# A decoder layer in three-product fp32 on one core: attention probabilities and half of the gated sum turned by VectorE and DMAs, and two of five FFN pairs computed by seven block products

## Chip, cores and metric

One core of a Trainium2 chip runs the whole layer in one launch. The metric is the device time of one execution in microseconds (us). The kernel before was timed three times, and its median is the number to compare with. Beside the times stands one profiled execution of the kernel before; all rows and durations come from it. Engines are named as the profile names them: PE (TensorE matmul), PEld (its weight loads), DVE (VectorE), ACT (ScalarE), POOL (GpSimd), SP (SyncE, which here only issues DMAs). SPq and ACTq are the queues on which SP and ACT issue DMAs.

## The reference

```python
h = rmsnorm(x, norm1_g)                       # x: 256 tokens x 1024
u = h @ w_in                                  # 1024 x 7168: rnn_x | rnn_gate | q | k | v | two gates
ya = rg_lru(causal_dwconv4(x_rnn)) * gelu(g_rnn)
yb = softmax(causal(rms(q) @ rms(k).T)) @ v   # 8 heads x 128; 256 tokens are one block
merged = sigmoid(g_A) * (ya @ w_proj_rnn) + sigmoid(g_B) * (yb @ w_proj_attn)
x = x + merged @ w_out
h = rmsnorm(x, norm2_g)
up = causal_dwconv3(h @ w_up)                 # 1024 x 2816
x = x + (gelu(up) * (h @ w_gate)) @ w_down    # 2816 x 1024
```

All of it is float32, with one sequence of 256 tokens and one layer.

## The kernel before, in words

**Matmuls.** Each float32 operand is split into two parts of type fp32r: `hi` is a cast (ACT), `lo` is the rest `raw - hi` (DVE). A product is three matmuls, hi*hi, hi*lo and lo*hi (`mm3`, line 424). The weights arrive as chunks of 128 x 2048 (1 MB). SP loads a chunk into `raw`, ACT casts it to `hi`, DVE subtracts to `lo`, and then PE runs 48 matmuls of 512 columns for two chunks of a 512-column weight block: 8 blocks of the inner dimension, 2 token tiles, 3 products. There are 3 buffers for `raw`, 4 for `hi` and 3 for `lo`.

**Stages.** The input projection runs in the order rx, rg, k, q, ga, v, gb with the recurrent gates `ri` between; attention (`att_s` line 772, `att_t` 797, `att_o` 807) is woven into ga, v, gb and pr; then come the projections pr and pa, the output projection `yo`, and the FFN. The FFN has five pairs: pair p is 512 columns of w_up and 512 of w_gate (`up`, `gt`), then a last half pair (`last`) and eleven chunks of w_down (`dn`, accumulated in `acc`).

**Turning.** PE leaves tokens on the partitions; the convolution and the next matmul want channels there. `turn` (line 446) does it without PE: one DVE transpose in 32 x 32 blocks, four DMAs that write the tile to DRAM with the blocks in order, and one DMA that reads it back. SP issues all five, and the read must wait until the writes have landed. The tiles q, k, rx, rg and all FFN outputs are turned so. Three other turns are done by PE with an identity matrix: the probabilities of a head (`pt`, three 128 x 128 transposes in `att_t`), the gated sum (`mT`, `m_t` line 860, four groups of four) and the second norm's input (`h2T`).

**Order.** The kernel's functions only record operations. `Later.issue` (line 283) then emits them in the order of the table `ORDER` (line 160): a number is a recorded operation of ACT, DVE, POOL or SP, and `+n` is the next n matmuls. Each engine runs its own instructions strictly in that order. As one line emits them all, every row of the profile carries L296, and groups are told apart by the names of their tiles.

Of the kernel before, what the change touches and what calls it, by code (L numbers as in the profile page):

```python
# [7 lines left out]
F32 = mybir.dt.float32  # L8
# [6 lines left out]
P = 128  # L15
S = 256
# [13 lines left out]
HALVES, SMALLS, WARM, RAWS = 23, 10, 11, 3  # L30
AHEAD_S, AHEAD_L = 2, 3
DVE_HI = (39, 42, 43)
KEPT = {"upd": 2, "gtd": 2, "u": 1, "c": 2, "ah": 3, "al": 3, "s": 1}
UNITS = ("rx0 rx1 rx2 rx3 rg0 rg1 rg2 rg3 k0 k1 k2 k3 ri0 q0 q1 ri1 ga0 ga1 q2 q3 v0 v1 ga2 ga3 v2 v3 gb0 "
         "gb1 gb2 gb3 pr0 pr1 pr2 pr3 pa0 pa1 pa2 pa3")
AFTER = {
    "rx0.0": "s4 stats",
    "rg0.0": "ev0",
    "rg0.3": "ev1",
    "rg1.1": "rx0",  # L40
    "rg1.2": "s5 rx1",
    "rg1.3": "s6 ge0",
    "rg2.1": "xo0",
    "rg3.0": "rgr0",
    "rg3.1": "conv0",
    "rg3.2": "xo1",
    "rg3.3": "s7 ge1",
    "k0.0": "s8 s9",
    "k0.2": "rgr1 conv1",
    "k1.2": "s10 s11",  # L50
    "k1.3": "s12",
    "k2.2": "s13",
    "k2.3": "split0 decay",
# [96 lines left out]
    "gt41.3": "ur4",  # L150
    "dn4.0": "fu4 s69",
    "dn4.1": "s70 fg3",
    "dn5.2": "lr5 gr4",
    "dn5.3": "s71",
    "dn7.0": "fu fg fg4",
    "dn8.0": "s73",
    "dn9.3": "s74",
}

ORDER = """  # L160
0-2 +1 3-4 +1 5 +1 6 +1 8 +1 7 +1 9 +1 11 +2 10 25 +1 12 30 +1 26-27 +1 14 +1 28 33 +1 29 +1 13 31 +2 32 +2 34 +2
35 +3 15 +6 36 +3 41 +3 19 +2 37 +1 63 42 +1 39 +4 43 38 +1 17 +1 40 +3 44 +1 49 +1 18 +3 45 +1 64 50 +1 47 +3 51
+1 48 +1 16 +1 46 +2 52 +2 57 +4 53 +1 58 +1 55 +3 59 +1 54 +1 56 +3 60 +8 66 +4 68 67 +6 69 +2 99 +3 65 +5 70 +1
100 +4 71 +6 72 98 +1 73 +1 74-75 +1 76 +1 77 +1 78 +1 104 79 +1 80 +1 81 +1 82-83 +5 84 +1 105 +2 85 +3 116 +4 86
# [49 lines left out]
952 +1 951 +1 953 +3 954 +3 956 +1 955 +2 958 +2 957 +2 959-961  # L214
"""


# [972 lines left out]
```

## Time and profile before

| | |
|---|---|
| median of 3 runs | 434.46 us (434.1 to 435.2) |
| span of the profiled execution | 432.3 us from its first to its last instruction |
| around the span, against the median | 434.46 - 432.3 = 2.1 us |
| instructions in the profile | 5409 |
| loaded from and stored to DRAM by DMA | 101.09 MB |

The span is what the views of the profile divide; the 2.1 us around it are taken as unchanged. "Busy" is the time in which at least one instruction of an engine is in flight. Matmuls overlap each other, so a matmul's own duration is longer than its share of PE's time: the share is read from start to start.

### The profile page before, as it was taken

The page shows a single profiled execution, that of the slowest core. Times are in us where ns is not written, and L with a number is a line of the kernel's source. Part 1 is how long each engine was busy: PE and PEld are TensorE (multiplying, and loading weights), DVE is VectorE, ACT ScalarE, POOL GpSimd, SP SyncE. Part 2 cuts the span into 40 slices and gives each one's busy share as a digit, 9 for nine tenths or more (in the row PEclk, how much of TensorE's full clock was granted, in tenths as well). Part 3 has the DMA queues.
Part 4 walks back from the last instruction along what each step waited for, and adds up shares of the span by engine and source line. Part 5 has one row for each costly group of instructions (what it writes and reads, how often), then busy time and mean ns, then how long its engine had stood idle before and what let it go on. Part 6 is the DMA issues. An engine that isn't in the chain of part 4 may idle for free.

```text
span 432.3 us, 5409 instructions
## 1 busy us (share of the span) xinstructions
PE 427.6 (99%) x1992; PEld 357.3 (83%) x1992; DVE 324.5 (75%) x417; ACT 271.2 (63%) x307; POOL 51.9 (12%) x101
## 2 busy tenths in 40 slices
PE   9999999999999999999999999999999999999996
PEld 8888888888887888888888888888888888888885
DVE  4867499899898999865666796587888667769633
ACT  5687596886999998853241364468566556456510
POOL 0022483567160000000000000000000000000000
PEclk9999999999999999999999999999999999999999
DMA  7997945999991844474453556898888688788402
GB/s 253 395 394 256 339 169 149 295 314 335 368 313 38 284 142 149 130 238 134 181 194 116 176 203 207 299 325 253 284 265 313 237 270 262 243 286 293 152 0 97
DMA packets 33833, 101.09 MB, mean 234 GB/s; under 512 B 3216, under 2 KB 14096, under 8 KB 30352
## 3 DMA queue, kind: packets, MB, share of 16 engines
q1 hardware_dynamic: 33664, 100.76, 69.1%
q8 instruction: 15, 0.25, 0.2%
q14 instruction: 10, 0.08, 0.0%
q10 hardware_dynamic: 144, 0.00, 0.0%
HBM read 89.74 MB, written 11.01 MB: 233 GB/s over the span
## 4 chain that ended last, share of the span: by engine, by line
PE 87%; DMA 5%; ACT 3%; DVE 2%; issue 2%; SPq 0%; ACTq 0%; DVEq 0%
PE acc L296 14%; PE up L296 13%; PE gt L296 13%; PE rx L296 5%; PE gb L296 5%; PE pr L296 5%; PE yo L296 5%; PE pa L296 5%; PE k L296 5%; PE rg L296 5%; DMA qm<-qd 3%; PE q L296 3%; PE last L296 3%; PE v L296 2%; DMA raw<-in_win_fm 2%
## 5 line engine op out<-in xcount | busy, mean ns | idle before, releaser
L296 DVE TENSOR_TENSOR lo<-raw,hi 128x2048 fp32r<-128x2048 f32 (+1 forms) x72 | 160.3, 2227 | 40.1 <-PE gt L296 10.5
L296 ACT CAST hi<-raw 128x2048 fp32r<-128x2048 f32 (+1 forms) x69 | 128.3, 1862 | 49.7 <-PE gt L296 11.8
L296 PE MATMUL up<-hi,h2h 128*128 128x512 f32 x80 | 31.3, 391 | 0.0
L296 PE MATMUL up<-hi,h2l 128*128 128x512 f32 x80 | 31.2, 389 | 0.0
L296 PE MATMUL up<-lo,h2h 128*128 128x512 f32 x80 | 31.1, 389 | 0.0
L296 PE MATMUL gt<-hi,h2h 128*128 128x512 f32 x80 | 31.1, 389 | 0.0
L296 PE MATMUL gt<-lo,h2h 128*128 128x512 f32 x80 | 31.1, 389 | 0.0
L296 PE MATMUL gt<-hi,h2l 128*128 128x512 f32 x80 | 31.1, 389 | 0.0
L296 PE MATMUL acc<-hi,fah 128*128 128x512 f32 x80 | 31.1, 389 | 0.0
L296 PE MATMUL acc<-lo,fah 128*128 128x512 f32 x80 | 31.1, 389 | 0.0
L296 PE MATMUL acc<-hi,fal 128*128 128x512 f32 x80 | 31.1, 389 | 0.0
L296 POOL TENSOR_TENSOR rsq<-rsq 128x8 f32<-128x8 f32 x32 | 19.2, 600 | 28.6 <-DVE rsq L296 26.3
L296 ACT ACT_TABLE_LOAD x15 | 19.2, 1283 | 1.4 <-PEq L1180 1.2
L296 DVE SCALAR_TENSOR_TENSOR fc<-fu,pv,fc 128x255 f32<-128x255 f32 (+1 forms) x40 | 17.3, 477 | 2.1 <-ACT fc L296 2.1
L296 ACT ACTIVATE fc<-fu,pv 128x256 f32<-128x256 f32 x20 | 10.8, 593 | 11.1 <-DVE fu L296 11.1
L296 PEld LDWEIGHTS up<-hi,h2l 128*128 128x128 f32 x80 | 15.0, 188 | 3.2
L296 PEld LDWEIGHTS acc<-lo,fah 128*128 128x128 f32 x80 | 15.0, 188 | 3.1
L296 PEld LDWEIGHTS acc<-hi,fal 128*128 128x128 f32 x80 | 15.0, 188 | 3.1
L296 PEld LDWEIGHTS gt<-hi,h2l 128*128 128x128 f32 x80 | 15.0, 188 | 3.1
L296 PEld LDWEIGHTS gt<-lo,h2h 128*128 128x128 f32 x80 | 15.0, 188 | 3.1
L296 PEld LDWEIGHTS gt<-hi,h2h 128*128 128x128 f32 x80 | 15.0, 188 | 3.1
L296 PEld LDWEIGHTS acc<-hi,fah 128*128 128x128 f32 x80 | 15.0, 188 | 3.1
(222 smaller groups left out, 1038.8 us busy)
## 6 DMA issues: line engine op xcount, KB each, us to landing
raw<-in_win_fm SPq DMA_DIRECT2D x12, 1024.0 KB, 7.6
raw<-in_win_tm SPq DMA_DIRECT2D x12, 1024.0 KB, 7.2
raw<-in_wdown SPq DMA_DIRECT2D x11, 1024.0 KB, 6.7
raw<-in_wup SPq DMA_DIRECT2D x10, 1024.0 KB, 5.3
raw<-in_wgate SPq DMA_DIRECT2D x10, 1024.0 KB, 7.3
raw<-in_wpr SPq DMA_DIRECT2D x4, 1024.0 KB, 4.8
raw<-in_wpa SPq DMA_DIRECT2D x4, 1024.0 KB, 4.9
raw<-in_wout SPq DMA_DIRECT2D x4, 1024.0 KB, 4.8
```

The source lines that it names most:

```text
L296: getattr(engine, name)(*map(real, a), **{n: real(v) for n, v in k.items()})
```

## The change

1. **Probabilities.** `att_t` no longer uses PE. DVE transposes the 128 x 384 probabilities in blocks, SP writes them to DRAM in four DMAs, one DMA reads them back, and `att_o` reads the tile with a rearranged view. The 24 identity transposes are gone.
2. **Gated sum.** Its first half (g = 0) is turned by `turn` in `pa_evac`; the second half still uses PE (8 of 16 transposes are gone).
3. **Queue of the reads.** Every read-back of `turn` is issued by ACT (`TURN_ACT = "r"`); the writes stay on SP.
4. **FFN pairs 1 and 3** are computed as a 2 x 2 block product with seven block products instead of eight. The token halves and the two halves of the inner dimension are the blocks of the left operand, up and gate with the two halves of the inner dimension those of the right one. `forms` makes four sums of the left blocks once (for both pairs); `group` makes the sums of weight blocks, two by DVE additions of 128 x 2048 and two by DMAs that POOL issues and that add 1 MB from DRAM onto a loaded chunk. Each of the seven products needs its own split. Three weight chunks are loaded per group, the fourth comes in through the two adding DMAs.
5. **Smaller edits.** The copy of a turned `up` tile moves from DVE to ACT (`FU`); three casts that DVE did (`DVE_HI`) go to ACT; `raw` has 4 buffers instead of 3, the pool of 128 x 1024 tiles 21 instead of 23, the evacuated FFN tile `s` 2 instead of 1; all PSUM banks form one pool of 8. `ORDER` is another table.

```diff
-HALVES, SMALLS, WARM, RAWS = 23, 10, 11, 3
-DVE_HI = (39, 42, 43)
-KEPT = {"upd": 2, "gtd": 2, "u": 1, "c": 2, "ah": 3, "al": 3, "s": 1}
+HALVES, SMALLS, WARM = 21, 10, 11
+BUFS = {"raw": 4, "hi": 4, "lo": 3}
+SUMS = "dvdv"
+TURN_ACT = "r"
+KEPT = {"upd": 2, "gtd": 2, "u": 1, "c": 2, "ah": 3, "al": 3, "s": 2}
 ORDER = """
-0-2 +1 3-4 +1 5 +1 6 +1 8 +1 7 +1 9 +1 11 +2 10 25 +1 12 30 +1 26-27 +1 14 +1 28 33 +1 29 +1 13 31 +2 32 +2 34 +2
...
+0 2 1 3 +3 5 +4 6 +3 8 +1 7 9 11 10 12 14 13 24 15 29 17 25 18 28 +1 26 +1 32 27 +2 30 +3 31 +2 33 +3 34 +9 35 +3 40
...
-        item[read] = lambda: nc.sync.dma_start(dst, mid)
+        (nc.scalar if "r" in TURN_ACT else nc.sync).dma_start(dst if back is None else back, mid)
...
     def att_t(h):
-        sm = heads[h]
-        ps = bank(f"pt{h}")
-        for b in range(3):
-            nc.tensor.transpose(ps[:, b * P:(b + 1) * P], sm[:, b * P:(b + 1) * P], ident)
-        pth, ptl = small(f"pth{h}", 384, F32R), small(f"ptl{h}", 384, F32R)
-        split2(pth, ptl, ps[:, :3 * P])
+        turn(f"pm{h}", small(f"pd{h}", 384), probs[h], 3, probs[h])
+        a = small(f"ph{h}", 384, F32R), small(f"pl{h}", 384, F32R)
+        split2(*a, probs[h])
...
+    def forms(name, hi_, lo_, m, new):
...
+        nc.vector.tensor_sub(r1, a11, a10)
+        nc.vector.tensor_sub(s3, a00, a10)
+        nc.vector.scalar_tensor_tensor(s2, r1, -1.0, a00, op0=OP.mult, op1=OP.subtract)
+        nc.vector.scalar_tensor_tensor(s4, a01, -1.0, s2, op0=OP.mult, op1=OP.subtract)
+        for n, v in (("R1", r1), ("S4", s4), ("S2", s2), ("S3", s3)):
+            h, l = new(f"{name}{n}h"), new(f"{name}{n}l")
+            split2(h, l, v)
...
+    def group(name, a, src, rs, nrs, out0, out1, cols=True):
...
+        def add(n, to, tile_, dram_):
+            if by[n] == "v":
+                nc.vector.tensor_add(to, to, tile_)
+            elif dram_ is None:
+                nc.gpsimd.dma_start(to, tile_, accum_op=OP.add)
+            else:
+                nc.gpsimd.dma_start(to.rearrange("p (c n) -> p c n", c=2) if cols else to, dram_, accum_op=OP.add)
+
+        product(ps["a"], a["a00"], part("b00", x), True)
+        nc.scalar.activation(o[1][0], ps["a"], AF.Copy, scale=r[0])
+        nc.scalar.activation(o[0][1], ps["a"], AF.Copy, scale=r[1])
...
+        add("1", x, y, src[0][1])
+        product(ps["c"], a["R1"], part("t1", x), True)
...
+        product(ps["a"], a["a01"], part("b10", w), False)
...
+        product(ps["c"], a["S4"], part("b11", z), False)
...
+        add("2", x, z, src[1][1])
+        product(ps["b"], a["S2"], part("t2", x), True)
...
+        add("4", w, x, None)
+        product(ps["d"], a["a11"], part("t4", w), True)
...
+            add("3", z, None, src[0][1])
...
+        product(ps["b"], a["S3"], part("t3", y), False)
```

Each `product` is 12 matmuls of 512 columns (4 blocks of the inner dimension, 3 products). In the changed order's rows, `hif1b00`, `hif1t1` and so on are the hi parts of pair 1's plain blocks (b) and sums (t), `rawf1x`, `rawf1w` and `rawf1z` its three loaded chunks, and `hfR1`, `hfS2`, `hfS3`, `hfS4` the sums of the left operand. The changed kernel emits from another line, so its rows carry L180 where those of before carry L296.

For the two places of which the prediction speaks, the rows before and after follow. First DVE around FFN pair 1. Before, `lo47` to `lo50` are the lo parts of the chunks of pair 1 (and the first of pair 2), `fupd` and `fgtd` the turned outputs:

```order
L296 TENSOR_TENSOR lo47_2395<-raw47_2307,hi47_2360 128x2048
L296 STREAM_TRANSPOSE fupd0_2415<-fs0_2391 128x8x4x32
L296 TENSOR_TENSOR lo48_2434<-raw48_2339,hi48_2398 128x2048
L296 STREAM_TRANSPOSE fgtd0_2451<-fs0_2391 128x8x4x32
L296 TENSOR_TENSOR lo49_2475<-raw49_2373,hi49_2443 128x2048
L296 TENSOR_TENSOR lo50_2507<-raw50_2411,hi50_2478 128x2048
L296 STREAM_TRANSPOSE fupd1_2524<-fs0_2391 128x8x4x32
```

After, at the same place of DVE's list (the names are those of the paragraph above):

```order
L180 TENSOR_TENSOR lof1t1_2436<-rawf1x_2092,hif1t1_2396 128x2048
L180 TENSOR_TENSOR rawf1x_2092<-rawf1x_2092,rawf1z_2331 128x2048
L180 STREAM_TRANSPOSE fupd0_2464<-fs0_2449 128x8x4x32
L180 TENSOR_TENSOR lof1b11_2472<-rawf1z_2331,hif1b11_2439 128x2048
L180 TENSOR_TENSOR lof1b10_2495<-rawf1w_2369,hif1b10_2474 128x2048
L180 STREAM_TRANSPOSE fgtd0_2512<-fs0_2449 128x8x4x32
L180 TENSOR_TENSOR rawf1w_2369<-rawf1w_2369,rawf1x_2092 128x2048
L180 TENSOR_TENSOR hfS4l_2532<-h201_2335,hfS4h_2431 128x512
L180 TENSOR_TENSOR lof1t2_2538<-rawf1x_2092,hif1t2_2505 128x2048
L180 TENSOR_TENSOR hfS2l_2552<-h200_2254,hfS2h_2423 128x512
L180 TENSOR_TENSOR lof1t4_2560<-rawf1w_2369,hif1t4_2544 128x2048
L180 TENSOR_TENSOR lof1t3_2582<-rawf1z_2331,hif1t3_2568 128x2048
```

Where DVE had four subtractions of 128 x 2048 for the pair, it now has seven of them and two additions of the same size, with two splits of the left operand's sums between them.

Second ACT in the attention stage, from the probabilities of the first heads on. Before (`sm` are a head's probabilities, `pth` the hi part of the turned ones, `hi26` a weight chunk):

```order
L296 ACTIVATE qTh1_1338<-qd1_1147 128x1024
L296 CAST pth3_1347<-pt3_1312 128x384
L296 CAST hi26_1354<-raw26_1192 128x2048
L296 ACTIVATE sm0_1349,mx0_1350<-sm0_1349,mx0_1350,rq0_1089 128x128
L296 ACTIVATE sm0_1349,mx0_1350<-sm0_1349,mx0_1350,rq0_1089 128x256
L296 CAST pth1_1383<-pt1_1364 128x384
```

After (`pm` is the copy in DRAM, `ph` the hi part of the turned probabilities, `higb` a weight chunk):

```order
L180 CAST higb0_1317<-rawgb0_1114 128x2048
L180 DMA sm3_1196<-pm3_1271 128x384
L180 ACTIVATE sm1_1267,mx1_1268<-sm1_1267,mx1_1268,rq0_1008 128x128
L180 ACTIVATE rt0_726<-rt0_726 128x1024
L180 ACTIVATE a20_1348<-rt0_726 128x1024
L180 DMA sm2_1242<-pm2_1315 128x384
L180 ACTIVATE sga1_1364<-ga10_1216,rs1_282 128x512
L180 CAST higb1_1369<-rawgb1_1173 128x2048
L180 CAST ph3_1388<-sm3_1196 128x384
```

The read of a turned tile now stands in ACT's own list, ahead of the exponentials and the weight casts that follow it there; before, the list had no DMA in this stage.

More of the change, by code (lines that the diff above doesn't have):

```diff
@@ L397, in split_tiles @@
[L397 to L417 removed]
+              "pr": lambda c: two(wpr, 0, c), "pa": lambda c: two(wpa, 0, c),
@@ new lines, in trunk_layer, with load @@
+              "up": lambda c: two(wup, 0, c), "gt": lambda c: two(wgate, 0, c),
+              "last": lambda c: [w[NF - 1, :, c * 1024:(c + 1) * 1024] for w in (wup, wgate)],
+              "wo": lambda c: wout[c], "dn": lambda c: wdown[c]}
+    def load(name, src, pieces=1):
+        r = wp.tile([P, 2048], F32, tag="raw", name=f"raw{name}", bufs=BUFS["raw"])
+        if isinstance(src, list):
+            n = 2048 // len(src)
+            for a, v in enumerate(src):
+                nc.sync.dma_start(r[:, a * n:(a + 1) * n], v)
+        elif len(src.shape) == 3:
+            nc.sync.dma_start(r.rearrange("p (c n) -> p c n", c=2), src)
+        else:
+            n = src.shape[-1] // pieces
+            for a in range(pieces):
+                nc.sync.dma_start(r[:, a * n:(a + 1) * n], src[:, a * n:(a + 1) * n])
+        return r
@@ L419, in split2, with chunk @@
+    def chunk(kind, c, n=2048, **k):
+        return split(f"{kind}{c}", load(f"{kind}{c}", source[kind](c)), n, **k)
     def split2(dh, dl, src):
@@ L858, in pa_evac @@
             nc.vector.tensor_add(m, m, tok(sga, g, t))
+        if MT[g]:
+            d = half(f"md{g}")
+            turn(f"mm{g}", d, sgb.half(g))
+            v = lambda a: a.half(g).rearrange("p (c t i b) -> p t c i b", c=4, t=2, i=4)
+            d = d.rearrange("p (i t c b) -> p t c i b", i=4, t=2, c=4)
+            for t in range(2):
+                nc.scalar.copy(v(mh)[:, t], d[:, t])
+                nc.vector.tensor_sub(v(ml)[:, t], d[:, t], f(v(mh)[:, t]))
     def m_t(c):
@@ new lines, in unit @@
+    def unit(kind, c):
+        if kind == "ri":
+            w = chunk(kind, c, 1024)
+            for n4 in range(4):
+                ri(c, w, n4)
+                if n4 == 3:
+                    lru(c)
+                yield
+            return
+        w = chunk(kind, c)
+        g, kh = c // 2, c % 2
+        if not kh:
+            open_ps[kind] = [bank(f"{kind}{g}{t}") for t in range(2)]
+        ps = open_ps[kind]
+        for k4 in range(4):
+            tm_mm(ps, w, 4 * kh + k4, k4, *{"pr": (yah, yal), "pa": (ybh, ybl)}.get(kind, (xgh, xgl)),
+                  kind not in "qkv")
+            if kh and k4 == 3:
+                evac[kind](g, ps)
+            yield
@@ L1018, in trunk_layer, with ffn_out, pair_act @@
     turned, gated = {}, {}
-    def pair_up(p):
+    FU = nc.scalar.copy
+    def ffn_out(kind, p, s):
+        d = half("fld") if kind == "last" else keep(kind + "d", p)
+        turn(f"{kind}m{p}", d, s)
+        v = d.rearrange("p (i t c b) -> p t c i b", i=4, t=2, c=4)
+        turned["last" if kind == "last" else (kind, p)] = v
+        if kind == "last":
+            last_block()
+        elif ("up", p) in turned and ("gt", p) in turned:
+            pair_act(p)
+    def pair_act(p):
         d = turned["up", p]
@@ L1125, in trunk_layer @@
+    NP = NF // 2
+    for token in PLAN.split():
+        step(token)
     with tc.manual_schedule():
```

663 lines of the change are left out of this document (256 added, 407 removed), and 83 rows, old and new, of the table ORDER.

## Prediction

> **What bounds the kernel now.** The page comes first: which engine is in flight all the time, and how near the others are.
>
> ```profile
> span 432.3 us, 5409 instructions
> ...
> PE 427.6 (99%) x1992; PEld 357.3 (83%) x1992; DVE 324.5 (75%) x417; ACT 271.2 (63%) x307; POOL 51.9 (12%) x101
> ```
>
> PE is in flight for all but 5 us. That alone doesn't show that it works without gaps, since matmuls overlap. The chain that ended last, in order of time, does:
>
> ```profile
> 271.19 10.88 PE up L296 x48
> 282.07 10.88 PE gt L296 x48
> ...
> 390.87 36.72 PE acc L296 x162
> ```
>
> 48 matmuls of 512 columns take 10.88 us, 0.2267 us from start to start. The 162 of `acc` take 36.72 us, the same 0.2267 each, so in the FFN nothing but the number of matmuls sets the time. Next, the busy time by stage; the columns are PE, weight loads, DVE, ACT, POOL, clock, DMA share and GB/s:
>
> ```profile
> 86.00:150.00 64.00, 63.62 (x317) 53.54 (x316) 57.96 (x91) 58.17 (x74) 23.93 (x37) 1.00 0.82 278
> 150.00:190.00 40.00, 40.00 (x201) 33.55 (x200) 35.15 (x56) 35.77 (x45) 0.00 (x0) 1.00 0.49 163
> 190.00:250.00 60.00, 60.00 (x289) 49.92 (x287) 40.83 (x40) 19.22 (x22) 0.00 (x0) 1.00 0.47 158
> 250.00:290.00 40.00, 40.00 (x181) 33.13 (x180) 28.46 (x35) 22.50 (x24) 0.00 (x0) 1.00 0.80 264
> 290.00:330.00 40.00, 40.00 (x179) 33.10 (x178) 34.25 (x43) 26.38 (x27) 0.00 (x0) 1.00 0.88 288
> 330.00:370.00 40.00, 40.00 (x178) 33.14 (x177) 27.51 (x26) 23.59 (x22) 0.00 (x0) 1.00 0.73 239
> ```
>
> The clock is 1.00 throughout. In the attention stage (86 to 190) DVE has 93.1 and ACT 93.9 of 104 us: both are nearly full, and PE shows 0.4 us of idle time. In the FFN, DVE is at 69 to 86% and ACT at 56 to 66%. So the kernel is bound by PE, with DVE and ACT close behind where attention runs, and DMA at 0.73 to 0.88 in the FFN.
>
> **The change part by part: what PE loses.** Two groups of seven products have 84 matmuls each instead of 96: 2 x 12 x 0.2267 = 5.4 us. The identity transposes are priced from their place in the timeline of PE:
>
> ```profile
> 128.34 0.49 PE L296 MATMUL pt<-ident,sm 128*128 128x128 f32 x3
> 128.59 0.48 PE L296 MATMUL ga<-hi,xgh 128*128 128x512 f32 x1
> 128.91 0.40 PE L296 MATMUL ga<-lo,xgh 128*128 128x512 f32 x1
> ...
> 249.67 0.60 PE L296 MATMUL h2T<-ident,xs 128*128 128x128 f32 x4
> 250.03 0.48 PE L296 MATMUL up<-hi,h2h 128*128 128x512 f32 x1
> 250.34 0.39 PE L296 MATMUL up<-lo,h2h 128*128 128x512 f32 x1
> ```
>
> Three of them take 0.25 us up to the next matmul, which itself takes 0.32 instead of 0.23: 0.34 for a head, 2.7 us for eight. Four (of `h2T`, whose shape is that of `mT`) take 0.36 + 0.08 = 0.44; two such groups go, 0.9 us. Together PE loses 5.4 + 2.7 + 0.9 = 9.0 us, all of it on the path. That is the ceiling, but for the few tenths of idle time seen above.
>
> **What the two groups ask of DVE and ACT.** The durations:
>
> ```profile
> L296 DVE TENSOR_TENSOR lo<-raw,hi 128x2048 fp32r<-128x2048 f32 x68 | 155.5, 2287 | 38.8 <-PE gt L296 10.5 <-issue 9.1 <-PE rg L296 7.0
> L296 DVE STREAM_TRANSPOSE fupd<-fs 128x1024 f32<-128x1024 f32 x5 | 6.2, 1241 | 0.5 <-ACT fs L296 0.5
> L296 DVE STREAM_TRANSPOSE qd<-q 128x512 f32<-128x512 f32 x4 | 2.8, 710 | 0.4 <-ACT sqq L296 0.4
> L296 DVE SCALAR_TENSOR_TENSOR vl<-v,rs,vh 128x512 fp32r<-128x512 f32 x4 | 2.8, 747 | 0.1
> L296 DVE TENSOR_TENSOR fc<-fgtd,fc 128x512 f32<-128x512 f32 x10 | 6.5, 687 | 4.2 <-DMA fgtd<-gtm 3.0 <-ACT fc L296 1.2
> L296 DVE SCALAR_TENSOR_TENSOR fc<-fu,pv,fc 128x254 f32<-128x254 f32 x20 | 8.5, 475 | 0.0
> L296 DVE COPY fu<-fupd 128x512 f32<-128x512 f32 x10 | 3.8, 418 | 5.6 <-DMA fupd<-upm 5.6
> L296 ACT ACTIVATE fs<-up,rs 128x512 f32<-128x512 f32 x10 | 6.9, 686 | 7.0 <-PE up L296 6.9
> ```
>
> *Pair 1.* In DVE's new list, from the lo part of pair 0's last chunk to `lof1t3`, stand nine instructions of 128 x 2048 (seven subtractions, two additions), two transposes, six subtractions of 128 x 512 and two scalar-tensor ones: 9 x 2.287 + 2 x 1.241 + 6 x 0.687 + 2 x 0.747 = 28.7 us. In the same stretch PE has 48 matmuls of pair 0 and six products, 120 x 0.2267 = 27.2 us. DVE is 1.5 us too long before it has waited for anything. ACT has a wait of its own there: the third product adds onto the bank of the first, which ACT must have copied twice; its second copy stands behind the copy of the second product's bank, so PE waits for two copies, 2 x 0.686 = 1.4 us. DVE works on in that time, so the two don't add. With handovers I take 2.0 us.
>
> *Pair 3.* From the first addition to the lo part of the w_down chunk that follows the group: eight of 128 x 2048, eight convolution steps, two products of 128 x 512 and one scalar-tensor: 8 x 2.287 + 8 x 0.475 + 2 x 0.687 + 0.747 = 24.2 us. PE has 14 + 84 matmuls, 22.2 us. The evacuations stand early in ACT's list here. I take 2.0 us.
>
> Both could cost less, since DVE's durations overlap by some hundredths each, or up to 4 if every handover is seen; the range keeps 0.5 to 4 for each.
>
> **Attention.** DVE gets eight transposes of 128 x 384; between zero and the 0.71 of 128 x 512, by size 0.53, 4.3 us in all: 93.1 + 4.3 = 97.4 of 104 - 2.7 = 101.3 us. ACT gets 13 reads to issue. The nearest row of an issue by ACT, and the time that the writes before a read need:
>
> ```profile
> L296 ACTq DMA_DIRECT2D g<-in_vec x1: 405/405/405, 0.7 to 0.7; - x1
> ...
> upm<-fupd SPq DMA_DIRECT2D x20, 128.0 KB, 6.1
> gtm<-fgtd SPq DMA_DIRECT2D x20, 128.0 KB, 6.6
> ```
>
> 13 x 0.405 = 5.3 us, so ACT has 99.2 of 101.3 us. Both engines go from 90% to 96 and 98%; from nothing (the gaps just fill) to 5.3 us (all of it seen). The share of PE time lost at 90% was nearly none, so I take 1.5 us.
>
> **The reads' queue.** SP no longer stands still until a turned tile's writes have landed:
>
> ```profile
> SPq L296 <- DMA gtm<-fgtd: 15.4, 9, 3.9
> SPq L296 <- DMA upm<-fupd: 13.9, 9, 5.0
> ```
>
> These 29.3 us held weight loads up but not PE, which had no gap in the FFN, so their end is worth nothing, at best the 0.4 us of idle time in attention. [...]
>
> **The adding DMAs.** No row shows one. The nearest are plain loads of the same 1 MB:
>
> ```profile
> raw<-in_wup SPq DMA_DIRECT2D x10, 1024.0 KB, 5.3
> raw<-in_wgate SPq DMA_DIRECT2D x10, 1024.0 KB, 7.3
> ```
>
> Between a DMA's issue and the cast that waits for it, the new order has 37 matmuls and four transposes (8.8 us), 39 (8.8), 60 (13.6) and 34 (7.7). The slack behind the casts adds 2.9 us to the first, 1.1 to the second and 2.2 to the last. So landings up to 9.9 us are hidden at all four. If they cost what plain loads do, the price is 0; at twice the slower row, 14.6 us, it is 2.9 + 4.7 + 0 + 4.7 = 12.3 us. I take 0, nearer to the loads, as it moves the same bytes from DRAM. [...]
>
> **At nothing:** the ten copies of `fu` move from DVE (0.418 each) to ACT, hidden by ACT's idle 13 to 17 of 40 us in the FFN, 6 us if that cover were gone. The three casts that ACT takes over lie where it has 19 of 60 us. The fourth `raw` buffer can only help.
>
> **Sum:** -9.0 + 2.0 + 2.0 + 1.5 = -3.5 us. The profiled execution's span would go from 432.3 to 428.8, and with the 2.1 us around it the time is 434.46 - 3.5 = 431.0 us.
>
> **The rivals.** About 0.3%, 1.3 us, can be told from no change: faster is below 433.2, slower above 435.8.
>
> *All hidden.* DVE and ACT keep up, and the whole 9.0 us or most of it shows: 425.5 to 428.2. For it: PE ran without a gap beside DVE at 91%. Against it: the two sums above exceed PE's time.
>
> *ACT's list takes it all back.* A read waits in ACT's order until the writes have landed. The new order has 13 to 20 matmuls between the last write and the read for four heads (3.6, 3.6, 4.4 and 4.6 us). If those writes land like those of `upm`, after 6.1 us, ACT stands still for 2.5 + 2.5 + 1.7 + 1.5 = 8.2 us, with exponentials and weight casts behind it. ACT then has 107.4 us of work in 101.3, a loss of 6 in place of my 1.5: 435.5 us. It matters once these waits exceed some 4 us. Against it: the probabilities' writes are smaller (48 KB, not 128).
>
> *The adding DMA is slow* (slower than before). It reads its target as well as its source, so it may take twice a load. Every microsecond over 9.9 delays `t3` in both groups, over 11.7 also `t1` in pair 1, and DVE, which has no slack there, stands behind it. It ends above 435.8 from a landing of 12.1 us on (2 x 2.2 + 0.4 = 4.8 us); midway between 10.6 and 14.6, at 12.6, it costs 6.3 us: 437.3.
>
> **How the numbers follow.** Some of the gain given back (428.2 to 433.2, at 431.0): 0.44. All hidden: 0.18. Taken back by ACT's list (433.2 to 435.8): 0.18. Slow adding DMA: 0.20. So faster 0.62, same 0.18, slower 0.20. The range leaves out the last half microsecond of the best case and landings above some 12.8 us: 426.0 to 438.0. The likeliest case's own range is 428.2 to 433.2.
>
> **What would show it.** Right: 56 matmuls fewer on PE; 0.2267 us from start to start in the products; DVE above 95% around both groups, and PE waiting for DVE's `lof` tiles and for ACT's copy of `f1a`, some 2 us in each group. Wrong: PE without gaps in the groups (all hidden); waits of ACT's queue for `pm` tiles of over 4 us in all, and PE idle at the heads; a landing of the POOL-issued DMAs above 10 us with casts of `t1` or `t3` waiting for it; DVE durations beside these DMAs unlike those quoted.

## The result, and the profile after

The changed kernel takes 438.38 us (median of 4 runs, 436.57 to 439.78), the kernel before 434.39 (4 runs, one more than ahead of the prediction, 434.1 to 435.2): 1.0086 times as long, 95% interval 1.0057 to 1.0115. A later measurement of the same kernel gives 438.79 us and 1.0113 (1.0086 to 1.0139). The prediction said 431.0 and 426 to 438, so both the sign and the range were wrong. The ratios here and below leave out single executions far above the rest, while the medians keep them (603.3 us in e5, 1501.29 in e13 and 2413.75 in e15 of the experiments, 465.1 in the kernel before).

The profiled execution is the fastest of the four: 436.57 us with a span of 434.8, 2.5 us longer than before. First the page, then PE's waits (engine and tile, what it waited for, total, times, longest):

```profile
span 434.8 us, 5465 instructions
PE 422.0 (97%) x1936; PEld 349.7 (80%) x1936; DVE 352.2 (81%) x439; ACT 292.9 (67%) x330; POOL 56.1 (13%) x105
```

```profile
PE pr L180 <- DVE yal L180: 2.7, 1, 2.7
PE f1b L180 <- ACT fc L180: 2.4, 1, 2.4
PE f1a L180 <- ACT fs L180: 1.4, 1, 1.4
PE f3b L180 <- DVE fs L180: 1.2, 1, 1.2
```

The 56 matmuls are gone. But PE, which waited once for 0.4 us before, now waits at four places for 7.7 us: once in the attention stage, three times in the groups.

**This wait costs more than itself.** The timeline of PE around the first of them, and the same stretch by windows (columns as before; the clock is the third number from the end):

```profile
175.18 0.39 PE L180 MATMUL pr<-lopr,yah 128*128 128x512 f32 x1
178.26 0.50 PE L180 MATMUL pr<-hipr,yal 128*128 128x512 f32 x1 [2.69 <-DVE yal L180]
...
179.35 0.63 PE L180 MATMUL pr<-hipr,yah 128*128 128x512 f32 x1
179.78 0.63 PE L180 MATMUL pr<-lopr,yah 128*128 128x512 f32 x1
180.20 0.63 PE L180 MATMUL pr<-hipr,yal 128*128 128x512 f32 x1
```

```profile
178.00:180.00 2.00, 1.74 (x6) 1.41 (x7) 2.00 (x4) 1.98 (x2) 0.00 (x0) 0.80 0.03 8
180.00:182.00 2.00, 2.00 (x6) 1.51 (x6) 1.96 (x4) 1.99 (x6) 0.00 (x0) 0.50 0.21 51
182.00:184.00 2.00, 2.00 (x9) 1.66 (x8) 2.00 (x5) 2.00 (x3) 0.00 (x0) 0.84 0.64 157
```

A microsecond after PE resumes, its matmuls start every 0.43 us instead of 0.2267: the granted clock is 0.50 (called half clock below). Seven of them at that pace and one on either side cost another 1.6 us.

**The attention stage.** Why `yal` is late is plainest in the second profile of the same kernel (span 436.3 us), where a wait of PE for `ybl` comes ahead of it. Timelines of ACT, DVE and PE, one row each:

```profile
166.82 0.33 ACTq L180 DMA_DIRECT2D sm<-pm  x1
167.18 1.28 ACT L180 ACT_TABLE_LOAD   x1 [4.35 <-DMA pm<-pd]
```

```profile
169.82 0.42 DVE L180 TENSOR_TENSOR ybl<-o,ybh 128x256 fp32r<-128x256 f32 x1 [4.06 <-ACT ybh L180]
```

```profile
170.30 0.39 PE L180 MATMUL o<-ph,vh 128*128 128x256 f32 x1 [2.45 <-DVE ybl L180]
```

ACT comes to the read of a head's probabilities, whose writes haven't landed, and stands for 4.35 us. The cast `ybh` is behind it, so DVE stands for 4.06 us, and then PE for 2.45. One wait goes through three in-order lists.

**Pair 1.** ACT, DVE and the chain of waits, in the profile of the changed kernel ahead of the last product (`t3`):

```profile
284.11 0.69 ACT L180 ACTIVATE fs<-f1a,rs 128x512 f32<-128x512 f32 x1
287.50 0.33 ACTq L180 DMA_DIRECT2D fgtd<-gtm  x1
287.93 1.91 ACT L180 CAST hif1t<-rawf1z 128x2048 fp32r<-128x2048 f32 x1 [3.12 <-PE f1b L180]
```

```profile
289.87 2.29 DVE L180 TENSOR_TENSOR lof1t<-rawf1z,hif1t 128x2048 fp32r<-128x2048 f32 x1 [3.33 <-ACT hif1t L180]
292.08 0.74 DVE L180 SCALAR_TENSOR_TENSOR fs<-f1b,rs,fs 128x512 f32<-128x512 f32 x1
```

```profile
280.25 7.16 DMA gtm<-fgtd
```

The name behind the 3.12 us is PE, and that behind PE's own 2.4 us is ACT's `fc`; but `fc` ended only after PE had started (the second profile names DVE's `fs` for the same wait), and the last write of `gtm` lands at 287.41 and the read goes out at 287.50: ACT had been standing at the read since 284.8, with the cast of `t3` behind it. DVE waits for the cast, makes the lo part, and only then empties bank b, onto which PE adds the last product: PE starts at 292.97, just after 292.08 + 0.74. The group therefore waits for a place in two lists, not for a sum of durations. In pair 3 only the second half of this is left: the evacuation stands behind the lo part, and DVE comes to it late, since it works without a gap from 325.4 us on.

The wait of 1.4 us at `f1a` is for ACT's second copy of that bank. It stands right behind the copy of bank c, and PE resumes at 279.22, when both are done:

```profile
277.90 0.69 ACT L180 ACTIVATE fs<-f1c,nrs 128x512 f32<-128x512 f32 x1
278.49 0.68 ACT L180 ACTIVATE fs<-f1a,rs 128x512 f32<-128x512 f32 x1
```

The second copy can't stand earlier in the list, since it writes a buffer of `s` that holds pair 0's gate tile until DVE has turned it. Here that was done at 278.37, before the copy's turn came; in the profile of e3 below ACT waits 0.85 us for it, and PE 2.3.

### The profile page after: what moved, and what is told of

Read it like the earlier page. It is cut to its first block, busy times and chain, and to the rows that moved or that the text cites. A ratio compares the mean times of both kernels' runs of the same rounds, so it can differ in the third digit from the quotient of the medians.

```text
span 434.8 us, 5465 instructions
## 1 busy us (share of the span) xinstructions
PE 422.0 (97%) x1936; PEld 349.7 (80%) x1936; DVE 352.2 (81%) x439; ACT 292.9 (67%) x330; POOL 56.1 (13%) x105
## 4 chain that ended last, share of the span: by engine, by line
PE 76%; DVE 9%; DMA 9%; ACT 2%; issue 2%; SPq 1%; ACTq 0%; DVEq 0%
PE acc L180 13%; PE gt L180 8%; PE up L180 7%; PE pr L180 5%; PE pa L180 5%; PE q L180 5%; PE k L180 5%; PE rg L180 5%; PE yo L180 5%; PE rx L180 4%; DMA pm<-pd 3%; PE ga L180 3%; PE last L180 3%; PE v L180 2%; DMA gtm<-fgtd 2%
## 5 line engine op out<-in xcount | busy, mean ns | idle before, releaser
L180 PE MATMUL acc<-hidn,fal 128*128 128x512 f32 x80 | 31.2, 389 | 0.0
L180 PE MATMUL acc<-lodn,fah 128*128 128x512 f32 x80 | 31.1, 389 | 0.0
L180 PE MATMUL acc<-hidn,fah 128*128 128x512 f32 x80 | 31.1, 389 | 0.0
L180 DVE TENSOR_TENSOR lodn<-rawdn,hidn 128x2048 fp32r<-128x2048 f32 x11 | 25.1, 2283 | 4.9 <-issue 4.9
L180 ACT CAST hidn<-rawdn 128x2048 fp32r<-128x2048 f32 x11 | 20.9, 1901 | 1.0 <-PE last L180 1.0
L180 POOL TENSOR_TENSOR rsq<-rsq 128x8 f32<-128x8 f32 x32 | 17.7, 552 | 14.2 <-DVE rsq L180 12.0
L180 PE MATMUL up<-hiup,h2h 128*128 128x512 f32 x48 | 19.0, 396 | 0.0
L180 PE MATMUL up<-hiup,h2l 128*128 128x512 f32 x48 | 18.8, 392 | 0.0
L180 PE MATMUL up<-loup,h2h 128*128 128x512 f32 x48 | 18.7, 390 | 0.0
L180 PE MATMUL gt<-higt,h2h 128*128 128x512 f32 x48 | 18.7, 389 | 0.0
L180 PE MATMUL gt<-logt,h2h 128*128 128x512 f32 x48 | 18.7, 389 | 0.0
L180 PE MATMUL gt<-higt,h2l 128*128 128x512 f32 x48 | 18.7, 389 | 0.0
L180 POOL DMA_DIRECT2D rawf1x<-in_wgate x1 | 1.4, 1392 | 126.4 <-DVE ss L180 126.4
L180 PEld LDWEIGHTS acc<-hidn,fal 128*128 128x128 f32 x80 | 15.0, 188 | 3.3 <-DVE fal L180 0.2
L180 PEld LDWEIGHTS acc<-hidn,fah 128*128 128x128 f32 x80 | 15.0, 188 | 3.1
L180 PEld LDWEIGHTS acc<-lodn,fah 128*128 128x128 f32 x80 | 15.0, 188 | 3.1
L180 DVE SCALAR_TENSOR_TENSOR fc<-fu,pv,fc 128x255 f32<-128x255 f32 (+1 forms) x40 | 16.7, 474 | 0.0
L180 ACT CAST hiwo<-rawwo 128x2048 fp32r<-128x2048 f32 x4 | 7.7, 1916 | 12.4 <-PE pa L180 7.5
L180 PE MATMUL pr<-hipr,yal 128*128 128x512 f32 x32 | 13.2, 412 | 2.7 <-DVE yal L180 2.7
L180 ACT CAST higt<-rawgt 128x2048 fp32r<-128x2048 f32 x6 | 11.5, 1914 | 5.0 <-DVE fc L180 3.5
L180 DVE TENSOR_TENSOR logt<-rawgt,higt 128x2048 fp32r<-128x2048 f32 x6 | 13.7, 2283 | 0.0
```

Source lines behind the costliest of these rows:

```text
L180: getattr(engine, name)(*map(real, a), **{n: real(v) for n, v in k.items()})
```

## Experiments

The theories. **A**, lists: ACT stands at reads, and instructions that PE needs stand behind others. **B**, load: DVE (with ACT) has more work than PE leaves it time for. **C** is named where it is used. **D**: the adding DMAs. All have 5 rounds, with the kernel before on the same chip; e1 to e4, e5 to e8, e9 to e11, e12 to e15 and e16 ran on one chip each, where the kernel before had medians of 434.45 to 434.74 us. One number recurs: what PE lost in a stage, worked out from the trace as the sum of what the times from a 512-column matmul's start to the next start exceed 0.2267 us. "Attention" is ga, v, gb and pr, "groups" the products of pairs 1 and 3 and `acc`. Half clock is included. These losses are those of the one profiled execution, which can lie well off the median: 433.20 us in e4 (median 437.71), 437.03 in e1, 438.28 in e5, 435.51 in e7.

| kernel | median, us | ratio to before (95%) | attention | groups |
|---|---|---|---|---|
| before | 434.39 | 1 | 2.2 | 0.0 |
| changed | 438.38 | 1.0086 (1.0057 to 1.0115) | 5.4 | 6.5 |
| changed, again | 438.79 | 1.0113 (1.0086 to 1.0139) | 7.1 | 6.2 |
| e1 reads on SP | 434.71 | 1.0004 (0.9978 to 1.0030) | 4.7 | 6.5 |
| e3 probabilities on PE | 435.82 | 1.0024 (1.0011 to 1.0037) | 1.5 | 7.8 |
| e4 plain DMAs | 437.71 | 1.0078 (1.0051 to 1.0104) | 3.8 | 4.4 |
| e5 moves in the groups | 436.47 | 1.0051 (1.0025 to 1.0076) | 8.4 | 5.4 |
| e6 yal first | 439.80 | 1.0135 (1.0109 to 1.0160) | 6.2 | 7.8 |
| e7 all moves | 438.06 | 1.0083 (1.0062 to 1.0105) | 4.2 | 6.5 |
| e9 no additions | 437.98 | 1.0069 (1.0046 to 1.0093) | 8.1 | 5.3 |
| e10 no transposes | 437.25 | 1.0085 (1.0060 to 1.0110) | 5.1 | 6.3 |
| e11 PE, SP, moves | 433.77 | 0.9986 (0.9973 to 0.9998) | 1.4 | 5.5 |
| e12 moves, no additions | 435.38 | 1.0009 (0.9984 to 1.0034) | 8.0 | 3.7 |
| e13 no transposes, SP | 432.79 | 0.9959 (0.9932 to 0.9985) | 1.8 | 5.0 |
| e14 three adding DMAs | 442.56 | 1.0167 (1.0142 to 1.0192) | 1.5 | 13.4 |
| e15 SP, moves | 432.84 | 0.9953 (0.9934 to 0.9971) | 2.8 | 4.5 |
| e16 SP, moves, yal | 431.92 | 0.9943 (0.9923 to 0.9964) | 2.7 | 4.0 |

In executions that have the changed kernel's attention stage unaltered (the two above, e4, e5, e9, e12) that column goes from 3.8 to 8.4; a difference of 3 us there says little by itself. The groups' column without half clock (1.4 us of it in e1, e3 and e6) is 6.2 to 6.5 wherever that stage is unaltered and the reads stand on ACT. In kernels with moved or added instructions the rows carry L188 or L200 in place of L180.

**e1: the reads on SP again.**

```diff
-TURN_ACT = "r"
+TURN_ACT = ""
```

> All read-backs of turned tiles go to SP's queue again; nothing else changes. Theory A (lists: the time is lost where ACT stands at a read until the writes have landed, and where an instruction that PE needs stands behind another in an engine's order): ACT's waits for pm, gm and gtm end, the gap of 2.7 us ahead of the first pr product and the slow clock of 1.6 us behind it shrink to under 1 us together, and PE's wait at the last product of pair 1 falls from 2.4 to about 1 us; 438.4 - 5 = 433 to 434.5 us, unless SP, which now stands at the reads, brings weight chunks too late (rows of ACT waiting for raw chunks would show it). Theory B (load: DVE and ACT have more work than PE leaves them time for, wherever the reads stand): gaps at pr and in the groups stay, 437.5 to 439 us.

The median falls by 3.7 us, to that of the kernel before, 0.2 above A's range. PE's waits in its profile:

```profile
PE f3b L180 <- DVE fs L180: 2.3, 1, 2.3
PE pr L180 <- DVE yal L180: 1.9, 1, 1.9
PE f1a L180 <- ACT fs L180: 1.4, 1, 1.4
```

The wait at `t3` of pair 1 is gone. But 1.9 us stay at `pr`, where A allowed under one, and pair 3 waits longer than it did; both are followed by half clock in this execution. In pair 3 DVE now stands for the cast of `t3`, which ACT began after standing 3.5 us itself, until the adding DMA had landed:

```profile
341.09 2.29 DVE L180 TENSOR_TENSOR lof3t<-rawf3z,hif3t 128x2048 fp32r<-128x2048 f32 x1 [1.03 <-ACT hif3t L180]
```

Reads on ACT are the dearest single piece, and not the only one. SP's longest waits stay those for DVE to free chunk buffers (35.9 us for `logt`, 33.8 in the changed kernel).

**e3: the probabilities turned by PE.** `att_t` is as before the change, with its transposes ahead of the cast; writes, read and DVE's transpose are gone. The lines are shortened; in the run a helper puts the transposes at their place in `ORDER`.

```diff
-        turn(f"pm{h}", small(f"pd{h}", 384), probs[h], 3, probs[h])
+        for b in range(3):
+            nc.tensor.transpose(ps[:, b * P:(b + 1) * P], sm[:, b * P:(b + 1) * P], ident)
```

> The probabilities of all heads are turned by PE again (24 transposes, placed ahead of the cast that reads them), so DVE's eight transposes, 32 writes and 8 reads are gone; the rest of the change stays. PE gets 2.7 us more. Both theory A and theory B say that the gap of 2.7 us at pr and the 1.6 us of slow clock go, since ACT loses the waits at the reads and DVE 4.3 us of work: 438.4 + 2.7 - 4.3 = 436.8 us, so this part of the change is worth about nothing. Theory C (the gap at pr comes from the rest of the new order, not from the turned probabilities): the gap stays, 441 us. The FFN's waits of 5.0 us stay in all three.

435.82, and every wait in the attention stage is gone (1.5 us lost there, less than before the change), though PE has 24 transposes more. So in the changed kernel the probabilities' way through DRAM cost some 2.6 us net. C (the rest of the new order) falls: it isn't the cause there. The runs spread over 1.3 us, those of the changed kernel over 3.2.

**e4: plain instead of adding DMAs.**

```diff
-    nc.gpsimd.dma_start(to.rearrange("p (c n) -> p c n", c=2) if cols else to, dram_, accum_op=OP.add)
+    nc.gpsimd.dma_start(to.rearrange("p (c n) -> p c n", c=2) if cols else to, dram_)
```

> The four DMAs that POOL issues write their 1 MB plainly instead of adding it, so the sums t1 and t3 hold one block instead of the sum of two. Theory D (the adding DMA is what costs the groups their time): landing falls from 8.4 to 10.6 us to some 5 to 7, and PE's waits in the groups fall by 2 us or more; 436.4 us or less. Theories A and B: the landing doesn't decide any wait of PE, and the time stays within 1 us of 438.4 us.

The adding DMAs of the changed kernel, and the plain ones, with size and us to landing:

```profile
rawf1x<-in_wgate POOLq DMA_DIRECT2D x1, 1024.0 KB, 10.6
rawf1z<-in_wgate POOLq DMA_DIRECT2D x1, 1024.0 KB, 9.3
rawf3x<-in_wgate POOLq DMA_DIRECT2D x1, 1024.0 KB, 8.7
rawf3z<-in_wgate POOLq DMA_DIRECT2D x1, 1024.0 KB, 8.4
```

```profile
rawf1x<-in_wgate POOLq DMA_DIRECT2D x1, 1024.0 KB, 7.2
rawf1z<-in_wgate POOLq DMA_DIRECT2D x1, 1024.0 KB, 6.9
rawf3x<-in_wgate POOLq DMA_DIRECT2D x1, 1024.0 KB, 7.0
rawf3z<-in_wgate POOLq DMA_DIRECT2D x1, 1024.0 KB, 5.8
```

Adding takes 1.2 to 1.5 times as long, as D had it, and the median falls by 0.7 us, as A and B had it. In the first profile of the changed kernel no wait of PE goes back to one of these DMAs; ACT stands about 2 us for the last of them (issue at 331.32, cast at 339.85; the same in the second profile), but DVE is busy until after that, and PE's wait there is the same 1.2 us in e4. In the profile of e4, the fastest of its six runs, the groups lose 2 us less all the same, the amount that D named: ACT's stand at the read before `t3` is 1.14 us instead of 3.12, since the turned gate tile's writes landed earlier. From the start of DVE's transpose to that read 10.1 to 10.4 us pass in the five profiles with adding DMAs and the same work and order there (the two of the changed kernel, e3, e6, e10), and 8.4 in e4. That the adding DMA slowed those writes is likely from this, not shown.

**e2 and e5: moves in the groups.** e2 moved four instructions. Two of the moves were too far: one read bank b ahead of its last two matmuls, and one overwrote the gate tile of pair 0 before DVE had turned it, so those parts of the output are wrong and its 437.21 us (1.0048, 1.0023 to 1.0073) tell of another program.

> Four instructions of the FFN groups change places in their engine's order: the read of the turned gate tile goes behind the cast of t3 (ACT), the evacuation of bank b goes ahead of the lo part of t3 in both groups (DVE), the second copy of bank a goes ahead of the cast of t2 (ACT). Theory A (lists): PE's waits in the groups, 1.4 + 2.4 + 1.2 = 5.0 us, fall to 1 us or less; 438.4 - 4 = 434.4 us (433.5 to 435). Theory B (load on DVE): DVE is as late as before, the waits move to other products and at least 3 us of the 5.0 stay; 436.5 to 438.4 us. Nothing changes ahead of the FFN in either.

e5 has three moves that keep every dependence (numbers of `ORDER`; the run lists the moves in a table, and the lines show the order that comes out):

```diff
-... 740 +2 785 ...
+... +2 785 740 ...
-... 786 ... 779 ...
+... 779 786 ...
-... 900 ... 893 ...
+... 893 900 ...
```

On ACT, 740 is the read of the gate tile and 785 the cast of `t3` (pair 1). On DVE, 786 is the lo part of `t3` and 779 the evacuation of bank b; 900 and 893 are the same two in pair 3.

> Three moves in the FFN groups: ACT's read of the turned gate tile of pair 0 goes behind the cast of t3, and the lo part of t3 goes behind the evacuation of bank b in pair 1 and in pair 3 (DVE). Theory A (lists): PE's waits at the last product, 2.4 and 1.2 us in the profile of the changed kernel, fall to 0.3 us or less each; the wait for the second copy of bank a (1.4 us) stays. Time 3.5 us below the changed kernel itself, which is run beside it. Theory B (load on DVE): what is moved ahead makes something else late by as much; at least 2 us of the 3.6 stay as waits elsewhere in the groups.

The two waits of 2.4 and 1.2 us are gone, as A said; and others have come in pair 3 and at `acc`, as B said:

```profile
PE f1a L188 <- ACT fs L188: 1.4, 1, 1.4
...
PE acc L188 <- DVE fal L188: 0.6, 1, 0.6
PE f3a L188 <- DVE lof3b L188: 0.5, 1, 0.5
```

With gaps too short for these rows the groups lose 5.4 instead of 6.2 to 6.5 us: a gain of 1 out of 3.6. The median is 2.3 us below that of the changed kernel on the same chip, between A's 3.5 and B's 1.6 at most.

**e6: yal first.** In DVE's order the lo part of the first gated half (594) goes right behind 356, ahead of head 6's scaling and transposing and of the second half's four scans (357 to 360).

```diff
-... 356 ... 547 ... 549 ... 357 ... 358 ... 359 ... 360 ... 594 ...
+... 356 594 ... 547 ... 549 ... 357 ... 358 ... 359 ... 360 ...
```

> One move in DVE's order: the lo part of the first gated half (yal 0) goes ahead of the scaling and transposing of head 6 and of the four scans of the second half. Theory A (lists): PE's wait of 2.7 us ahead of pr falls to 0.5 us or less and the slow clock behind it is gone; 3 to 4 us below the changed kernel. Theory B (load on DVE in the attention stage): the scans come 1.2 us later and yal 1 with them, the wait reappears at the second half of pr or at pa, and the gain is under 1.5 us.

439.80: nothing gained. The wait moves to the second half of `pr`, 22 matmuls on: 2.0 us for ACT's `yah`, and 1.1 in two waits for `yal`, one of them at the old place. B.

**e7 and e8: all moves; the changed kernel again.** e7 adds a third buffer `s`, so that the second copy of bank a can stand right behind the first; that move and those of e5 and e6 are in it too.

```diff
-KEPT = {..., "s": 2}
+KEPT = {..., "s": 3}
...
-    s = [keep("s", n) for n in range(2)]
+    s = [keep("s", n + 1) for n in range(2)]
```

> All four moves of the two kernels above, and a third buffer for the evacuated FFN tile, so that the second copy of bank a in pair 1 no longer waits until DVE has transposed pair 0's gate tile; that copy then stands right behind the first. Theory A: all of PE's waits in the middle of the kernel (2.7 + 1.4 + 2.4 + 1.2 = 7.7 us) and the slow clock behind them go: 438.4 - 7.7 - 1 = about 429.5 us, which beats both kernels, and the times of its runs spread less than the 3 us of the changed kernel. Theory B: at least half of it comes back as other waits of PE for DVE, 433 us or more.

> The changed kernel itself, for comparison on the same chip. Both theories: 437 to 439 us. If the slow clock of TensorE behind a wait comes by chance, the place and number of stretches at half clock differ between this profile and the first one of the same kernel, at the same waits; if it belongs to the program, they are the same.

438.06, far from A's 429.5. The wait at `f1a` is gone and `f3a` has one:

```profile
PE pr L188 <- ACT yah L188: 2.0, 1, 2.0
PE f3a L188 <- DVE lof3b L188: 1.7, 1, 1.7
...
PE acc L188 <- DVE fal L188: 0.9, 2, 0.5
PE pr L188 <- DVE yal L188: 0.6, 1, 0.6
```

e8 has the same four waits as the first profile, and the one for `ybl` shown above; half clock came behind that one (granted clock 0.50 from 172 to 174 us), and not behind the 2.1 us at `pr` (1.00 from 178 to 184 us). So its place isn't the program's.

**e9 and e10: less work for DVE, same order.** e9 cuts the four additions to 8 columns, e10 leaves the eight transposes out.

```diff
-                nc.vector.tensor_add(to, to, tile_)
+                nc.vector.tensor_add(to[:, :8], to[:, :8], tile_[:, :8])
...
-            nc.vector.transpose(v, at.rearrange("p (u j b) -> p u j b", u=u, j=4))
+            if name.startswith("pm"):
+                dst = at
+                nc.vector.memset(none, 0.0)
...
```

> The four additions of 128x2048 that DVE makes for the groups (t2 and t4 of both) are cut to 8 columns, so the sums are wrong there and DVE has 4 x 2.29 = 9.2 us less to do in the two groups; the order and all waits are as in the changed kernel. Theory B (DVE's load): PE's waits and slow stretches between the first product of pair 1 and the end of pair 3, some 6 us in the changed kernel, fall to 2 us or less, and the time to 434.5 us. Theory A (lists): the wait for the second copy of bank a (1.4), for the read ahead of t3 (2.2 to 2.4) and for the evacuation behind lo t3 (1.2) stay for the most part, 437 us or more.

> DVE's eight transposes of the probabilities are left out (a one-column memset stands in each one's place); the four writes and the read of each head stay, and write the untransposed tile, so the attention's output is wrong. DVE has 8 x 0.55 = 4.4 us less in the attention stage. Theory B (DVE's load): PE's waits between 160 and 190 us, 4.7 and 6.9 us with their slow stretches in the two profiles of the changed kernel, fall to 2 us or less: 434 to 435.5 us. Theory A (ACT standing at the reads): the waits stay within 1 us, 437.5 us or more, since each read still waits for its writes.

Neither is worth more than 1.5 us. e9 has 9.2 us less for DVE, and all three waits of the groups:

```profile
PE f1b L180 <- DVE fs L180: 1.5, 1, 1.5
...
PE f1a L180 <- ACT fs L180: 1.4, 1, 1.4
...
PE f3b L180 <- DVE fs L180: 0.9, 1, 0.9
```

The one in pair 3 has another reason here: ACT stands 3.0 us until the adding DMA has landed, and DVE, which now has time, 0.85 for ACT's cast. e10 still waits 2.3 us at `pr`. Now A is favoured, where e6 and e7 favoured B. No theory of one cause survives both.

**e12 and e13: both causes taken away together.** e12 is e9's cut with e7's moves in the groups, e13 is e10 with e1's reads on SP.

> The moves in the FFN groups with the third buffer, and DVE's four additions cut to 8 columns (the sums t2 and t4 are wrong), together; the attention stage is as in the changed kernel. In the two groups and the acc products behind them PE lost 6.3 us in the profile of the changed kernel, 5.3 with moves and 4.6 without additions. Theory AB (two limits at once: the order of the lists and DVE's load; each hides the other): both removed, under 1.5 us is lost there. Theory A or B alone: no better than the better of the two, 4 us or more. Theory C (DMA landing): 4 us or more, with casts waiting for raw chunks.

> Reads on SP and DVE's eight transposes of the probabilities left out together (the attention's output is wrong; the writes and reads stay). With one of the two, PE still waited 2.1 and 2.5 us at pr. Theory AB (ACT's list and DVE's load, each enough by itself): the wait at pr is under 0.7 us, no slow clock. Theory C (the round trip of a head's probabilities through DRAM, some 3 to 6 us for the writes and 4 for the read, is itself too long for the order): ACT waits for the turned tile (ph) and the wait at pr stays above 1.5 us.

In e13 PE has 0.2 us of wait left at `pr`, and no half clock; with one cure it had been 1.9 and 2.3. The C of this expectation, the round trip through DRAM, falls. In e12 all of pair 1's waits are gone (0.7 us of small gaps left), and what stays is behind pair 3:

```profile
PE acc L188 <- ACT fah L188: 0.9, 1, 0.9
PE acc L188 <- DVE fal L188: 0.5, 1, 0.5
```

The groups lose 3.7 us, with one cure 5.3 or more. AB holds for the attention stage. The groups have to be read by pair, with the same sums of lost time:

| kernel | pair 1 | pair 3 and `acc` |
|---|---|---|
| changed | 4.6 | 1.8 |
| e7 moves, third buffer | 1.3 | 5.2 |
| e9 no additions | 3.8 | 1.5 |
| e12 both | 0.7 | 3.0 |

Pair 1 is mostly a matter of the lists: the moves alone bring 3.3 of its 4.6 us. But they pass the loss on to pair 3 and what is behind it, less so where DVE has time. AB expected under 1.5 us in all, so the 3.0 have a third cause. A candidate is on record in the expectation of e12, as its theory C, casts that wait for raw chunks:

```profile
339.70 1.91 ACT L188 CAST hif3t<-rawf3z 128x2048 fp32r<-128x2048 f32 x1 [4.41 <-DMA rawf3z<-in_wgate]
```

ACT stands until the adding DMA of pair 3 has landed (2.0 us in the changed kernel), and then works without a pause up to the cast `fah`, for which `acc` waits. The chain of waits also has the chunk `rawdn` there, which landed at 341.49. e14 below makes these landings later; no kernel here makes them earlier together with both cures, so how much of the 3.0 us is theirs stays open.

**e11, e14, e15, e16: versions built from this.** e11 has e3's PE transposes, e1's reads, the third buffer and the moves of 786, 893 and 766 (the second copy of bank a). e15 is the same with the probabilities through DRAM. e14 is e11 with one more kind of sum by DMA:

```diff
-SUMS = "dvdv"
+SUMS = "dddv"
```

e16 is e15 with e6's move.

> A version put together from what the runs so far favour: probabilities turned by PE again, read-backs on SP's queue, the lo part of t3 behind the evacuation of bank b in both groups, and a third buffer so that the second copy of bank a comes right behind the first. From the changed kernel with the probabilities on PE (435.8): the second copy's wait of 1.4 to 2.3 us and its share of slow clock go, and the read no longer stands ahead of t3 (0.9 us). Theory A: 435.8 - 4 = 432 us, which beats both kernels. Theory B: DVE is still too full in the groups, some 3 us of the waits move to other products, 434.5 us or more.

> The repaired version (probabilities on PE, reads on SP, moves, third buffer: 433.8 us), with the sum t2 of each group made by an adding DMA from DRAM instead of DVE: DVE has 2 x 2.29 us less, two more DMAs of 1 MB are issued by POOL. If DVE's load is what is left in the groups, 1.5 to 3 us come back: 431 to 432.3 us. If the adding DMA's landing (8.4 to 10.6 us) is too long for the 7 us between the lo part of t1 and the cast of t2, that cast waits some 2 us in each group and PE about 1 us: 433.5 to 435 us.

> The repaired version with the probabilities turned through DRAM as in the change (reads on SP, moves, third buffer). Beside the repaired version with PE's transposes (433.8 us) it prices this part of the change: PE has 2.7 us less to do. If the part is worth what the count of matmuls says: 431 us. If the attention stage gives it back as in e1 (2.1 us of wait, 0.9 ahead of yo, and slow clock): 434 to 435.5 us.

> The version with reads on SP, the moves in the groups and the third buffer (432.8 us), with the lo part of the first gated half moved ahead of head 6's scaling and transposing and of the second half's scans on DVE. Theory AB (two limits at once; ACT's list is now free of reads): the wait at pr falls from 1.6 to 0.3 us or less, 431.5 us. DVE's load alone: as with reads on ACT, the wait comes back at the second half of pr (there 2.0 + 0.6 us), 432.5 us or more.

e11 just beats the kernel before; its 433.77 us are between the two expectations. e14 is 8.8 us slower than e11 (7.9 by the ratios to the kernel before, as the two ran on different chips), and neither of its expectations had that. The adding DMAs now land after 9.4 to 13.7 us (a row with x2 gives the median), ACT stands for the cast of `t2`, and the copy behind that cast is what PE waits for:

```profile
rawf1x<-in_wgate POOLq DMA_DIRECT2D x2, 1024.0 KB, 10.5
rawf3x<-in_wgate POOLq DMA_DIRECT2D x2, 1024.0 KB, 11.4
```

```profile
ACT hif1t L200 <- DMA rawf1x<-in_wgate: 6.2, 2, 3.6
ACT hif3t L200 <- DMA rawf3x<-in_wgate: 5.1, 1, 5.1
```

```profile
PE f3c L200 <- ACT fs L200: 3.4, 1, 3.4
PE f1c L200 <- ACT fs L200: 2.2, 1, 2.2
```

In these kernels an adding DMA cost PE nothing only where what stood behind its result in the lists of ACT and DVE had time to spare: in the changed kernel ACT waited 1.6 us for the one of 10.6 us, and PE not at all. e15 is 0.9953 (0.9934 to 0.9971) of the kernel before, and five of its six runs spread over 1.3 us. It is 0.9 us below e11 by the medians and 1.4 by the ratios (two chips): the turned probabilities are worth about 1 of the 2.7 us that the count of matmuls promised, where reads don't stand on ACT. e16 is the fastest, 431.92 us and 0.9943 (0.9923 to 0.9964), but the intervals of the two overlap. Its wait at `pr` is between the two expectations, 1.3 us in place of 1.6:

```profile
PE pr L188 <- ACT yah L188: 0.7, 1, 0.7
PE pr L188 <- DVE yal L188: 0.6, 1, 0.6
```

## Why the prediction was wrong, point by point

- **PE loses 9.0 us**: right. 56 matmuls fewer, 0.2267 us from start to start in the products.
- **Reads' queue, "at best the 0.4 us"**: the first step that failed. That SP's freed list is worth nothing is right. But the cost on ACT was counted as issue time, 13 x 0.405 (it is 0.33 each), and not as the time that ACT stands there with others behind it. Back on SP they are worth 3.7 us (e1), in the attention stage and at `t3` of pair 1.
- **Attention, 1.5 us**: 3.2 us more are lost than before in the first profile, 4.9 in the second, half clock included. The rival "ACT's list takes it all back" had the mechanism, with 8.2 us of standing and a loss of 6 in place of 1.5; it got 0.18. ACT's waits for the probabilities' writes and reads came to 4.6 us in the first profile and 7.5 in the second. Its end, 435.5, was too low since the pairs and half clock came on top. Against it the text held that 48 KB writes land sooner than 128 KB ones: they do at the median (3.1 us, where those of `gtm` take 5.7), but up to 6.2 here and 8.5 in the second profile.
- **Pair 1, 2.0 us**: 4.6. The two copies came out as 1.5 (1.4 predicted), for the reason predicted. That the two waits don't add was wrong: the other 2.5 us was put down to DVE's sum exceeding PE's by 1.5, and hidden behind the copies; e9 shows that 1.7 of it stays with 9.2 us less on DVE. It was the read ahead of the cast (on SP in e1, the wait is gone) and the evacuation behind the lo part. Comparing sums of durations can't see either.
- **Pair 3, 2.0 us**: 1.8, the size right, and in the changed kernel the reason too: DVE works without a gap from its first addition to the evacuation for which PE waits. The order has a part in it that the sum didn't see, the evacuation behind the lo part (e5).
- **The adding DMAs, 0**: right for PE's waits in the changed kernel. They land after 8.4 to 10.6 us (the plain ones of e4 after 5.8 to 7.2), where the text had hidden them up to 9.9; the one over that, 10.6, had ACT wait 1.6 us and PE not at all. The rival of the slow adding DMA is out as it was priced, from a landing of 12.1 us on. What they likely do to the gate tile's writes (not shown; up to 2 us in the groups, e4), and to pair 3 once ACT and DVE come to them sooner (1.0 us in e1), was not in the sum.
- **"The clock is 1.00 throughout"**: true of the kernel before, where PE waited once for 0.4 us, and not of the changed one: 0.50 behind the 2.7 us at `pr`, which added 1.6 us.
- **The sum**, by these measured terms: -9.0 + 3.2 + 4.6 + 1.8 + 0.9 (the start and the stages between) = +1.5; 0.7 more because the 9.0 counted the slower matmul behind each group of `pt`, which is in the 2.2 us of before as well. That is 2.2 of the 2.5 us that the span grew; the other 0.3 is not settled. Why the median lies 1.8 us above the profiled run isn't shown run by run; the second profile, 1.6 us above it in time, has a wait more.

What the experiments add: in the attention stage the changed order had two limits at almost the same place: one cure left about 2 us of wait at `pr`, both 0.2. In the groups a cure alone brought about 1 us or less in the profiles, and both 2.8, since what the moves gain in pair 1 comes back in pair 3 where DVE, and behind it an adding DMA, are the next limit.

## What to carry to other kernels

Price a DMA that an engine issues by how long the engine would stand at it and by what is behind it in its list, not by its issue time (a stand of 4.35 us in the second profile, 0.33 us of issue): put it on a queue whose engine has nothing else to do (SP here, 3.7 us less in e1). Where engines are full, compare places in the lists (bank to be emptied, buffer to be freed, cast behind a read) as well as sums, and when one cure brings nothing, try it together with the other before dropping it. In this kernel a gap of PE of 2 us and more is to be priced with another 1 us for the clock, an estimate: the 1.6 us at `pr`, in 13 cases of 21.

## What the runs showed of the hardware that was not expected

TensorE's clock after a gap: the 17 profiles of changed kernels have 21 gaps of 2.08 to 3.85 us (what the time from one matmul's start to the next exceeds 0.2267 us, so 0.2 above what the rows of waits give), and 13 were followed, 0.4 to 1.9 us after PE resumed, by 3 to 11 (mostly 7) matmuls at 0.427 us from start to start (granted clock 0.50 in the windows of the changed kernel, e1 and e8); none of the 17 gaps of 1.52 to 1.88 us was. Gaps of 2.53 (pair 1 in the changed kernel) and 2.78 us (e4) went without it and one of 2.08 (e1) had it, so a length alone doesn't decide. The usual length is 7 x 0.427 = 3.0 us; what sets it, and what decides between the gaps with and without it, is not shown. The half clock may be why the versions without gaps over 2 us (e11, e15, e16) spread over 1.3 to 2.1 us and the changed kernel over 3 to 4; that is argued from one profile each, and e3, whose profile has one such gap, spreads over 1.3 us too.

An adding DMA of 1 MB from DRAM onto SBUF took 1.2 to 1.5 times a plain one of the same queue (8.4 to 10.6 us in the changed kernel, 5.8 to 7.2 in e4). With two to a group they landed after 8.3 to 11.7 us in the 15 profiles that have them, with three (e14) after 9.4 to 13.7.
